# Asking for scratch stores through GpSimd's transfer queue instead of SyncE's

## The chip, the core and the metric

The kernel runs on one core of a Trainium2 chip. The core has a matrix engine (TensorE, in the profile PE, with its weight loads as PEld), a vector engine (VectorE, DVE), a scalar engine (ScalarE, ACT), GpSimd (POOL) and SyncE (SP). Each engine takes its own instructions strictly in order and waits on semaphores for the others. Transfers between the on-chip memory and the chip's main memory (HBM) are asked for by an instruction on one engine's queue, and are then carried by 16 DMA engines beside everything else. The metric is device time in microseconds of one execution.

## What is computed

One block of a streaming encoder on 1024 tokens of width 1024, all in float32, cut to what matters here:

```python
h = x + 0.5 * swiglu(rmsnorm(h, g1), W1)            # inner width 2816
u = rmsnorm(h, g2)
q, k, v, g_ret, p, gates = split(u @ w_in)          # 4 heads of 256
ret  = headnorm(retention(rotary(q), rotary(k), v)) * silu(g_ret)
pool = multiscale_pool(p, pool_w, pool_scale)       # trailing windows 2, 4, 8, 16
merged = sigmoid(gate0) * (ret @ w_ret_up) + sigmoid(gate1) * (pool @ w_pool_up)
h = h + merged @ w_out
h = h + 0.5 * swiglu(rmsnorm(h, g3), W2)
return rmsnorm(h, g_final)
```

## The kernel before

Activations lie on chip as tiles of 128 features by 1024 tokens. A float32 product is made of three matmuls: both operands are split into a high part, rounded to the matrix engine's format (ACT, line 161), and a low rest (DVE, line 162), and `mm3` (lines 181 to 183) multiplies high by high, high by low and low by high. Most matrix products are also cut by a Strassen scheme into seven block products instead of eight (`strassen`), and some into fewer still (`common`, lines 540 to 630). So DVE and ACT have much work beside PE: splits, sums and differences of blocks, and the evacuation of PE's result banks.

The stages run in this order: the first SwiGLU's inner products (`ffn_in`, tiles named `a...`), its outer product (`ffn_out`, `b...`), the projections (`values` with tiles `v...`, then `project` for q, k, g, p and the gates t), retention with the pooled branch's products as fillers (`retention`, `pool_up`), the merge (`two_groups`, `ru...`; `out_group`, `wo...`), the second SwiGLU (`c...`, `d...`), and the last norm.

Not everything fits on chip, so intermediate tiles go to scratch tensors in HBM and come back:

- `ffn_in` makes, for each of 11 pairs k of hidden tiles, four operands of the outer product and stores them: `B[k]` (`e["n"]`, line 797), `R[k]` and `T[k]` (`lo` and `hi`, after line 801), `T4[k]` (`e["m"]`, after line 806). `ffn_out` loads them: `p1` at first loads `R[k]` and then the weights `ra` (`bra`, `dra` in the trace); `p6` makes three sums of the weights on DVE (lines 906 to 908).
- `Next.quarter` keeps each new residual tile h (`h1` from `bacc`, `h2` from `wo`, line 311). The same tile is afterwards scaled in place by ACT (line 338, `r22`) and turned into operands.
- `project` stores q and k (`keep`), the swished g (`swish`), the two sigmoid gates (`gate`, line 1237, from small tiles `t0z` to `t7z`) and the pooled windows (`window`); `values` stores v, cut in rows of 1 KB (`store`).
- `pool_up` stores its gated product (`pm`), and the retention units their gated output (`ret`, line 1705).

Counted from the loops these are 88 stores in the two `ffn_in`, 32 of h, 16 of v, 16 of q and k, 8 of g, 32 of gates, 8 of pooled windows, 9 of `pm` and 8 of `ret`: 217, each of 256 or 512 KB.

All loads and all these stores go through one helper, `load` (line 140), which issues them on SP's queue. SP does nothing else. A store's tile lies in one of a few buffers that later tiles reuse, so whoever next writes the buffer waits until the store has landed.

What sets the order: the code states the work in a written order, in which `Flow` deals out side work between the matrix products. When the program is built, a planner places every instruction in its engine's queue by that order and by its own estimate of when the instruction can start; work under `soon()` goes first. On the chip each queue then runs in the order that was planned.

Of the kernel before, what the change touches and what calls it, by code (L numbers as in the profile page):

```python
# [90 lines left out]
def block_kernel(ctx: ExitStack, tc, x, x_tok, x_two, vecs, f1_in, f1_out, w_in, w_v, pool_w, w_ret, w_pool, w_o,  # L91
                 f2_in, f2_out, f2_far, g_row, rope, decay, consts, out, out_tok):
    nc = tc.nc
# [35 lines left out]
    def c2(name):  # L129
        return sb.tile([P, H], F32, tag="c2", bufs=N_C2, name=name)  # L130
# [7 lines left out]

    def load(dst, src):
        nc.sync.dma_start(dst, src)  # L140

    def eights(name):

        return sb.tile([P, 32], F32, tag="ss", bufs=2, name=name)[:, :8]
# [4 lines left out]
    def half(t, j):  # L149
        return t[:, j * H : (j + 1) * H]  # L150
# [146 lines left out]
    class Next(Norm):  # L297
# [9 lines left out]
        def quarter(self, mt, tokens, tile):  # L307
            src = tile[:, tokens]
            self.tiles[mt, tokens.start // H] = src
            if self.keep is not None:  # L310
                load(self.keep[mt][:, tokens], src)
            self.square(mt, tokens, src)

        def put(self, n, i, src, by=None):
# [426 lines left out]
    def ffn_in(nx, w, ops, name, start=None):  # L741

        R, T, B, T4 = ops
        hid = {}

        def group(g):
            gate_up = {}

            def dest(which):
                tile, j = which  # L750
                if tile not in gate_up:
                    gate_up[tile] = (tl if start and g == 0 else t4)(f"{name}{'gu'[tile]}{g}")
                return half(gate_up[tile], j)

            later = []

            def evac(which, in0, in1):
                tile, j = which
                dst, rms = dest(which), nx.rb
                if in1 is not None:  # L760
                    tt(dst, in0, in1, ADD)
                elif not tile and rms is not None:
                    tt(dst, in0, half(rms, j), MUL)
                    return
                else:
                    copy(dst, in0)
                if not tile:
                    later.append(j)

            def end():  # L770
                gate, up = gate_up[0], gate_up[1]

                def scale():
                    if len(later) == 2:
                        tt(gate, gate, nx.rms(), MUL)
                    else:
                        for j in later:
                            tt(half(gate, j), half(gate, j), half(nx.rms(), j), MUL)

                def times(j):  # L780
                    tt(half(up, j), half(gate, j), half(up, j), MUL)

                flow.add(scale, lambda: act(gate, gate, AF.Silu), lambda: times(0), lambda: times(1))
                hid[g] = up
                k = g % FH
                if g < FH:
                    return
                lo, hi, e = hid.pop(k), up, {}
                R11, R12, R21, R22 = half(lo, 0), half(lo, 1), half(hi, 0), half(hi, 1)

                def w1():

                    e["n"], e["m"] = gate, c2(f"{name}m{k}")
                    tt(half(e["n"], 0), R12, R11, SUB)

                def w1b():
                    tt(half(e["n"], 1), R22, R12, SUB)
                    load(B[k], e["n"])

                def w2():  # L800
                    tt(R12, R22, half(e["n"], 0), SUB)
                    load(R[k], lo)
                    load(T[k], hi)

                def w3():
                    tt(e["m"], R21, R12, SUB)
                    load(T4[k], e["m"])
                    done.add(k)

                flow.add(w1, w1b, w2, w3)  # L810

            if start and g == 0:
                return plain_group(nx, start, f"{name}{g}_", evac, end)
            return lambda shared: strassen(nx, w[g, 0], w[g, 1], f"{name}{g}_", evac, end, shared=shared, dest=dest)

        done = ops_done.setdefault(name, set())
        order = [g for k in range(FH) for g in (k, k + FH)]
        if start:

            return chain(group(0), pairs_of_both(nx, (group(g) for g in order[1:]), BY_OPERAND, 3))  # L820
        return pairs_of_both(nx, (group(g) for g in order), BY_OPERAND, 2)
# [320 lines left out]
    qs, ks, gs, pooled = (spill(n, KT) for n in ("q", "k", "g", "p"))  # L1142

    vs = spill("v", 4, 4 * H)
    gates = spill("gt", 2 * KT)
    pm, ret = spill("pm", KT), spill("ret", KT)
# [25 lines left out]
    def project(kind, n):  # L1172

        at = {"q": 0, "k": KT, "g": 3 * KT, "p": 4 * KT, "t": 5 * KT}[kind] + 2 * n
        name = f"{kind}{n}"
        pair = {}
# [44 lines left out]

        def keep(dst):
            for i in range(2):
                load(dst[2 * n + i], pair[i])
            stored.add(name)

        def swish(i):
            act(pair[i], pair[i], AF.Silu)
            load(gs[2 * n + i], pair[i])
            if i:  # L1230
                stored.add(name)

        def gate(i):
            mt = 2 * n + i
            for j in range(2):
                z = c2(f"{name}z{i}{j}")
                act(in_row(z), in_turns(half(pair[i], j)), AF.Sigmoid, bias=vec[:, V_B0 + mt : V_B0 + mt + 1])
                load(half(gates[mt], j), z)
            if i:
                stored.add(name)  # L1240

        def window(i):

            win = 2 << n
            t = {}

            def double(step):
                s = t.get("s", pair[i])
                o = t["s"] = t4(f"{name}s{i}_{step}")
                tt(o[:, step:], s[:, step:], s[:, : S - step], ADD)  # L1250
                copy(o[:, :step], s[:, :step])

            def mean():
                z, s = pair[i], t["s"]

                edge = sb.tile([P, 16], F32, tag="edge", bufs=2, name=f"{name}e{i}")
                tt(edge, s[:, :16], cst[:, C_CNT + 16 * n : C_CNT + 16 * n + 16], MUL)
                tt(edge, edge, z[:, :16], SUB)
                stt(s, s, 1.0 / win, z, MUL, SUB)
                copy(s[:, :16], edge)  # L1260
                load(pooled[2 * n + i], s)
                if i:
                    stored.add(name)

            return *(lambda b=b: double(1 << b) for b in range(n + 1)), mean
# [13 lines left out]
    def values():  # L1279
# [55 lines left out]

        def store(o, j, i, src):
            to = vs[2 * o + j].rearrange("p (h t c) -> p h t c", h=2, t=4)
            load(to[:, :, i], src.rearrange("p (h c) -> p h c", h=2))
            if i == 3:
                stored.update(f"v{h}{j}" for h in (2 * o, 2 * o + 1))  # L1340

# [101 lines left out]
    def pool_up():  # L1443
        gate, stores = {}, {}
        for mt in range(KT):

            def begin(mt=mt):
                await_stored(f"t{(KT + mt) // 2}")
                if mt < KT - 1:
                    r = raw(f"pg{mt}")  # L1450
                    load(r, gates[KT + mt])
                    gate[mt] = [half(r, j) for j in range(2)]
                    stores[mt] = [(pm[mt], r)]
                    return
                gate[mt] = [c2(f"pg{mt}{j}") for j in range(2)]
                for j, g in enumerate(gate[mt]):
                    load(g, half(gates[KT + mt], j))
                stores[mt] = [(half(pm[mt], j), g) for j, g in enumerate(gate[mt])]

            def evac(dst, mt=mt):  # L1460
                for j, g in enumerate(gate.pop(mt)):
                    tt(g, dst[j], g, MUL)
                for to, at in stores.pop(mt):
                    load(to, at)

            yield from plain(M.get, KT, w_pool[mt], f"pu{mt}", evac, begin,
                             (sum_bank, sum_bank if mt < 4 else bank))
# [41 lines left out]
    class Unit:  # L1509
# [185 lines left out]
        def finish(self):  # L1695
            for i in range(2):
                await_stored(f"g{self.h}")
                g = (t4 if self.h == 1 else tl)(f"rg{self.h}{i}")
                load(g, gs[2 * self.h + i])
                for nh in range(2):  # L1700
                    b = bank(f"ot{self.h}{nh}{i}")
                    for t in range(4):
                        o = t * HD + i * P
                        nc.tensor.transpose(b[:, t * P : (t + 1) * P], self.O[nh][:, o : o + P], ident)
                    tt(half(g, nh), b, half(g, nh), MUL)
                load(ret[2 * self.h + i], g)

    units = [Unit(h, nh) for h in range(NH) for nh in range(2)]
    up = Next("ru", None)
# [349 lines left out]
```

## Time and profile before

| | us |
|---|---|
| median of 3 runs | 2074.63 |
| lowest and highest of them | 2074.14, 2074.94 |
| the profiled execution, whole | 2073.32 |
| its span, first to last instruction | 2071.5 |
| outside the span | 1.8 |

| in the span | instructions on the engine | share of the span busy |
|---|---|---|
| PE matmuls | 10672 | 99% |
| PE weight loads | 10672 | 87% |
| DVE | 3262 | 89% |
| ACT | 2061 | 53% |
| transfers of SP's queue | 310.64 MB | 44.1% of the 16 DMA engines |

How to read the views: a row of the timeline gives start and duration in us, the engine, the line of the code, the operation, the tile that is written and those read, and in brackets how long the engine sat idle before it and what ended that. "SPq" is SP's queue; a row there is the issue of a transfer, not its movement. In the view of waits the three numbers are the total in us, how often, and the longest. Matmuls overlap, so a matmul's duration is longer than the step from one to the next.

### The profile page before, as it was taken

To read this page: it belongs to the slowest core of one execution; us is meant where nothing else is said; L and a number is where in the kernel's file an instruction comes from. 1 tells how busy PE (TensorE), PEld (TensorE's weight loads), DVE (VectorE), ACT (ScalarE), POOL (GpSimd) and SP (SyncE) were. 2 spreads that over 40 slices of the span, in tenths; PEclk is the share of its full clock that TensorE was granted. 3 is DMA by queue.
4 is the path that set the end of the run, shared out by engine and by line. 5 is a ranking of instruction groups with operands and counts; after the bars stand their busy time and mean duration, and the time that the engine had idled before them with its cause. 6 is when DMAs were issued, how large, how long until landed. Compare 5 with 4: busy or idle time off the path is not lost.

```text
span 2071.5 us, 29684 instructions
## 1 busy us (share of the span) xinstructions
PE 2046.9 (99%) x10672; PEld 1810.4 (87%) x10672; DVE 1835.4 (89%) x3262; ACT 1092.9 (53%) x2061; POOL 0.2 (0%) x4
## 2 busy tenths in 40 slices
PE   9999999999999999999999999999999999999998
PEld 7888999888888888888888999888789999988887
DVE  8799898997996799978878888999989989899897
ACT  8544454554653535444547763456645545455454
POOL 0000000000000000000000000000000000000000
PEclk9999999999999999999999999999999999999999
DMA  7232424585543333332436566724224232357642
GB/s 263 82 138 77 143 89 141 198 275 193 188 143 104 110 112 112 125 121 101 135 130 233 191 232 232 255 93 159 75 85 137 89 138 87 135 206 264 219 145 100
DMA packets 118819, 313.57 MB, mean 151 GB/s; under 512 B 13200, under 2 KB 17424, under 8 KB 118672
## 3 DMA queue, kind: packets, MB, share of 16 engines
q1 hardware_dynamic: 118096, 310.64, 44.1%
q8 instruction: 83, 1.36, 0.3%
q10 hardware_dynamic: 576, 1.05, 0.1%
q14 instruction: 64, 0.52, 0.1%
HBM read 220.93 MB, written 90.70 MB: 150 GB/s over the span
## 4 chain that ended last, share of the span: by engine, by line
PE 79%; DVE 15%; issue 2%; DMA 2%; ACT 1%; SPq 0%; ACTq 0%; DVEq 0%
PE c_b L181 2%; PE a_b L181 2%; PE c_b L182 2%; PE c_b L183 2%; PE a_b L182 2%; PE a_b L183 2%; PE c_e L183 2%; PE c_e L182 1%; PE c_e L181 1%; PE a_e L181 1%; PE a_e L183 1%; PE a_e L182 1%; PE c_a L183 1%; PE c_a L182 1%; PE c_a L181 1%
## 5 line engine op out<-in xcount | busy, mean ns | idle before, releaser
L182 PE MATMUL c_b<-n3T,c_wS 128*128 128x512 f32 x176 | 66.8, 380 | 0.0
L181 PE MATMUL c_b<-n3T,c_wS 128*128 128x512 f32 x176 | 66.5, 380 | 0.2 <-ACT n3T L161 0.2
L183 PE MATMUL c_b<-n3T,c_wS 128*128 128x512 f32 x176 | 66.7, 379 | 0.0
L181 PE MATMUL a_b<-n1T,a_wS 128*128 128x512 f32 x168 | 63.7, 379 | 0.0
L182 PE MATMUL a_b<-n1T,a_wS 128*128 128x512 f32 x168 | 63.7, 379 | 0.0
L183 PE MATMUL a_b<-n1T,a_wS 128*128 128x512 f32 x168 | 63.7, 379 | 0.0
L181 PE MATMUL a_a<-n1R,a_wL 128*128 128x512 f32 x120 | 45.5, 379 | 0.0
L183 PE MATMUL a_a<-n1R,a_wL 128*128 128x512 f32 x120 | 45.5, 379 | 0.0
L182 PE MATMUL a_a<-n1R,a_wL 128*128 128x512 f32 x120 | 45.5, 379 | 0.0
L182 PE MATMUL c_a<-n3R,c_wL 128*128 128x512 f32 x112 | 42.7, 381 | 1.1 <-DVE n3R L166 1.1
L181 PE MATMUL c_a<-n3R,c_wL 128*128 128x512 f32 x112 | 42.6, 380 | 0.7 <-ACT c_b L521 0.7
L183 PE MATMUL c_a<-n3R,c_wL 128*128 128x512 f32 x112 | 42.4, 379 | 0.0
L181 PEld LDWEIGHTS c_b<-n3T,c_wS 128*128 128x128 f32 x176 | 33.2, 189 | 5.1 <-ACT n3T L161 0.6
L182 PEld LDWEIGHTS c_b<-n3T,c_wS 128*128 128x128 f32 x176 | 33.3, 189 | 4.8 <-DVE n3T L162 0.3
L183 PEld LDWEIGHTS c_b<-n3T,c_wS 128*128 128x128 f32 x176 | 33.3, 189 | 4.6
L183 PEld LDWEIGHTS a_b<-n1T,a_wS 128*128 128x128 f32 x168 | 31.8, 189 | 4.5
L181 PEld LDWEIGHTS a_b<-n1T,a_wS 128*128 128x128 f32 x168 | 31.8, 189 | 4.4
L182 PEld LDWEIGHTS a_b<-n1T,a_wS 128*128 128x128 f32 x168 | 31.8, 189 | 4.4
L162 DVE TENSOR_TENSOR a_wS<-a_S,a_wS 128x512 fp32r<-128x512 f32 x45 | 30.6, 682 | 4.9 <-ACT a_wS L161 4.9
L161 ACT CAST c_wS<-c_S 128x512 fp32r<-128x512 f32 x46 | 27.8, 622 | 11.4 <-DVE c_S L484 7.0
L182 PE MATMUL c_e<-n3T,c_wL 128*128 128x512 f32 x88 | 33.5, 380 | 0.1
L181 PE MATMUL c_e<-n3T,c_wS 128*128 128x512 f32 x88 | 33.5, 380 | 0.0
(3159 smaller groups left out, 8002.1 us busy)
## 6 DMA issues: line engine op xcount, KB each, us to landing
c_ra<-in_f_in SPq DMA_DIRECT2D x22, 512.0 KB, 3.6
c_rb<-in_f_in SPq DMA_DIRECT2D x22, 512.0 KB, 3.8
a_ra<-in_f_in SPq DMA_DIRECT2D x21, 512.0 KB, 3.8
a_rb<-in_f_in SPq DMA_DIRECT2D x21, 512.0 KB, 3.8
t<-au SPq DMA_DIRECT2D x11, 512.0 KB, 2.8
b<-ag SPq DMA_DIRECT2D x11, 512.0 KB, 3.8
r<-au SPq DMA_DIRECT2D x11, 512.0 KB, 3.6
bra<-in_f_out SPq DMA_DIRECT2D x11, 512.0 KB, 5.4
```

What stands on the lines that cost most here:

```text
L161: copy(hi, src)
L162: tt(lo, src, hi.bitcast(F32), SUB)
L181: mm(dst, w[0], m[0], start=start, stop=False, skip_group_check=True)
L182: mm(dst, w[0], m[1], start=False, stop=False, skip_group_check=True)
L183: mm(dst, w[1], m[0], start=False, stop=stop, skip_group_check=True)
```

## The change

A second helper, `save`, issues a transfer on GpSimd's queue. The 217 stores into scratch memory call it instead of `load`. Loads stay on SP's queue, and so do the stores of the kernel's outputs (half of the token-major output stays on ACT's queue as before). No tile, buffer count, product or written order changes.

```diff
     def load(dst, src):
         nc.sync.dma_start(dst, src)
+
+    def save(dst, src):
+
+        nc.gpsimd.dma_start(dst, src)
...
             if self.keep is not None:
-                load(self.keep[mt][:, tokens], src)
+                save(self.keep[mt][:, tokens], src)
...
                     tt(half(e["n"], 1), R22, R12, SUB)
-                    load(B[k], e["n"])
+                    save(B[k], e["n"])
...
                     tt(R12, R22, half(e["n"], 0), SUB)
-                    load(R[k], lo)
-                    load(T[k], hi)
+                    save(R[k], lo)
+                    save(T[k], hi)
...
                     tt(e["m"], R21, R12, SUB)
-                    load(T4[k], e["m"])
+                    save(T4[k], e["m"])
...
-                load(dst[2 * n + i], pair[i])
+                save(dst[2 * n + i], pair[i])
...
-            load(gs[2 * n + i], pair[i])
+            save(gs[2 * n + i], pair[i])
...
-                load(half(gates[mt], j), z)
+                save(half(gates[mt], j), z)
...
-                load(pooled[2 * n + i], s)
+                save(pooled[2 * n + i], s)
...
-            load(to[:, :, i], src.rearrange("p (h c) -> p h c", h=2))
+            save(to[:, :, i], src.rearrange("p (h c) -> p h c", h=2))
...
                 for to, at in stores.pop(mt):
-                    load(to, at)
+                    save(to, at)
...
-                load(ret[2 * self.h + i], g)
+                save(ret[2 * self.h + i], g)
```

## The prediction

> **What bounds the kernel now.** First the page: its span, the busy shares and the chain of work that ended last.
>
> ```profile
> span 2071.5 us, 29684 instructions
> ...
> PE 2046.9 (99%) x10672; PEld 1810.4 (87%) x10672; DVE 1835.4 (89%) x3262; ACT 1092.9 (53%) x2061; POOL 0.2 (0%) x4
> ...
> PE 79%; DVE 15%; issue 2%; DMA 2%; ACT 1%; SPq 0%; ACTq 0%; DVEq 0%
> ```
>
> PE is busy for 2046.9 of 2071.5 us and carries 79% of the chain. DVE is next, and transfers are 2% of the chain. POOL does nothing. So an edit that removes no matmul can win at most the 24.6 us in which PE has none. The windows of 50 us tell where these lie.
>
> ```profile
> 0.00:50.00 50.00, 48.79 (x212) 39.62 (x213) 44.65 (x73) 43.55 (x78) 0.20 (x4) 1.00 0.75 262
> ...
> 400.00:450.00 50.00, 48.67 (x232) 42.63 (x231) 50.00 (x83) 25.67 (x44) 0.00 (x0) 1.00 0.79 268
> ...
> 1850.00:1900.00 50.00, 48.55 (x235) 42.61 (x235) 49.44 (x82) 25.36 (x44) 0.00 (x0) 1.00 0.77 269
> ...
> 2050.00:2071.50 21.50, 14.22 (x66) 11.83 (x64) 15.41 (x36) 7.91 (x19) 0.00 (x0) 0.94 0.51 195
> sum 2071.50, PE 2046.93 PEld 1810.45 DVE 1835.45 ACT 1092.90 POOL 0.20; mean PE 48.74 PEld 43.11 DVE 43.70 ACT 26.02 POOL 0.00
> ```
>
> The columns are length, then busy time and instructions of PE, PEld, DVE, ACT and POOL, then granted clock, share of the DMA engines and GB/s. PE lacks 1.2 us in the first row and 7.3 in the last, neither of which has a store into scratch near it. Some 16.1 us are left inside. The second and third row are the passage from `ffn_in` to `ffn_out` in the two SwiGLUs: 1.3 and 1.5 us missing there. In the view of PE's waits the largest, with what ended them, are:
>
> ```profile
> PE wo1b L181 <- ACT wo1wS L161: 1.7, 1, 1.7
> PE c_x L181 <- DVE cg L619: 1.5, 1, 1.5
> PE a_x L181 <- DVE ag L619: 1.3, 1, 1.3
> ...
> PE c_a L182 <- DVE n3R L166: 1.1, 2, 1.0
> ```
>
> PE waits for DVE or ACT, never for a transfer. A transfer counts only where DVE or ACT stood still for it just before.
>
> **Part 1: what stood behind a store.** The timeline of SP's queue at the two passages:
>
> ```profile
> 388.42 1.28 SPq L140 DMA_DIRECT2D bL22a<-in_f_out  x2
> 392.61 0.33 SPq L140 DMA_DIRECT2D m<-am  x1
> 392.99 0.93 SPq L140 DMA_DIRECT2D bra<-in_f_out  x2
> ...
> 1840.51 1.44 SPq L140 DMA_DIRECT2D dL22a<-in_f_out  x2
> 1844.71 0.33 SPq L140 DMA_DIRECT2D m<-cm  x1
> 1845.09 0.92 SPq L140 DMA_DIRECT2D dra<-in_f_out  x2
> ```
>
> And DVE's, around the first and at the second:
>
> ```profile
> 391.30 0.68 DVE L907 TENSOR_TENSOR bs<-bs,bra 128x512 f32<-128x512 f32 x1
> 391.91 0.68 DVE L806 TENSOR_TENSOR am<-au,au 128x512 f32<-128x512 f32 x1
> 392.51 0.68 DVE L908 TENSOR_TENSOR bs<-bra 128x512 f32<-128x512 f32 x1
> ...
> 398.22 0.69 DVE L906 TENSOR_TENSOR bs<-bra,bL22a 128x512 f32<-128x512 f32 x1 [1.42 <-DMA bra<-in_f_out]
> ...
> 1850.56 0.69 DVE L906 TENSOR_TENSOR ds<-dra,dL22a 128x512 f32<-128x512 f32 x1 [1.66 <-DMA dra<-in_f_out]
> ```
>
> SP had nothing to do from 389.70 (388.42 + 1.28). It stood at the store of `am` until DVE had made it (391.91 + 0.68 = 392.59). The weights `bra` behind it went out at 392.99, 0.05 us after the store's issue ended, so they waited for nothing of their own just then. DVE stood still 1.42 us for them, and PE missed 1.3 us soon after. The second passage is the same, with 1.66 and 1.5. With the store on POOL's queue SP goes straight on, and the weights can be asked for up to 3.3 us earlier (392.99 - 389.70), more than either idle time. What is late next is DVE itself, which is busy 50.00 of 50 us in that window. I take the whole of what PE missed, 1.3 + 1.5 = **2.8 us less**. The bounds are 0 (the buffer of `bra` free only just before) and 2.8.
>
> The other loads that stood behind stores had consumers that came later or that PE did not wait for, so I put nothing for them.
>
> **Part 2: the stores themselves.** They do not start earlier. The view of SP's own waits shows it standing at the stores:
>
> ```profile
> SPq L140 <- DVE am L806: 25.2, 11, 8.4
> SPq L140 <- DVE wo L1831: 23.9, 8, 8.5
> ...
> SPq L140 <- DVE wo L1833: 17.3, 8, 2.9
> ...
> SPq L140 <- DMA pm<-pg: 13.6, 6, 4.7
> ```
>
> For 11 of 11 stores of `am` and 16 of 16 of h from `wo` (two groups of eight), SP was there first and waited for the data. Such a store was issued 0.02 us after its data (392.59, 392.61) and gains nothing. What changes is how fast it lands from another queue. Rows of issues, the last number being the median from issue to landing:
>
> ```profile
> v<-vc SPq DMA_DIRECT2D x16, 256.0 KB, 3.4
> ...
> h<-wo SPq DMA_DIRECT2D x16, 256.0 KB, 2.0
> ...
> out<-n4o ACTq DMA_DIRECT2D x4, 256.0 KB, 2.6
> out<-n4o SPq DMA_DIRECT2D x4, 256.0 KB, 2.3
> ```
>
> No row has a store on POOL's queue. The nearest is the same output on ACT's and on SP's queue: 0.3 us later on the other one. The far end is what a store of the same size pays for a harder form, v against h: 1.4 us. That it lands sooner is bounded by the issue that SP's sequencer does, about 0.32 us:
>
> ```profile
> L140 SPq DMA_DIRECT2D h<-bacc x16: 319/323/327, 522.3 to 618.0; - x16
> ```
>
> So a store lands between 0.3 us sooner and 1.4 us later. I take the middle of the two late ends, 0.9 us, and keep both.
>
> A late landing costs only where someone waits for the tile. The gates are the clearest: one of those who waited for their stores, ACT's timeline, and PE's; below them ACT and DVE where they waited for h and v.
>
> ```profile
>   ACT g0p L543: 1.6, 1
> ...
> 778.55 1.57 ACT L1237 ACTIVATE t0z<-t0B,vec 128x512 f32<-128x512 f32 x2
> 780.02 0.57 ACT L526 COPY p3v<-p3b 128x512 f32<-128x512 f32 x1
> ...
> 780.64 0.48 PE L181 MATMUL p3b<-n2T,p3wS 128*128 128x512 f32 x1 [0.53 <-ACT p3v L526]
> ...
> 1415.97 0.72 ACT L338 ACTIVATE wo<-wo,vec 128x512 f32<-128x512 f32 x1 [0.27 <-DMA h<-wo]
> ...
> 660.03 1.39 DVE L1356 TENSOR_TENSOR vc<-vL,vf 128x512 f32<-128x512 f32 x2 [0.25 <-DMA v<-vc]
> ```
>
> Behind a sigmoid that waits for its small buffer stand, on ACT, the evacuations of PE's banks (lines 526, 543); PE missed 0.53 us for one. I find four such places: the gates that are made between the pooled groups (here, and once more in a later group), the scaling in place of h by ACT (line 338), which must wait for the store of the same tile, and v, where DVE waits for small tiles. At each, 0.9 us more meets some idle time of ACT or DVE; no row tells how much, so between all of it absorbed and none I charge PE one half: 4 x 0.9 / 2 = **1.8 us more**. Elsewhere PE has its distance: three matmuls on each of four tiles of a block product stand between a bank's last matmul and its next use.
>
> Stores that are read back (`pm` in the row above, `ret`) are late by the same 0.9 us, at 6 loads where SP waits for `pm`. DVE and ACT have their splits planned ahead of PE there, so I put nothing and leave it to the range.
>
> **Part 3: the queues.** SP is rid of 217 issues of about 0.32 us, some 70 us. Its share of the chain is 0%, so that is worth nothing by itself. POOL gets 217 issues and their waits, and has 2071 us for them; if it took the far end above, 1.4 us, for each, that is 304 us. Nothing else is queued there, so a store that waits for its data holds up only later stores, as it did on SP.
>
> **The sum.** 2073.32 - 2.8 + 1.8 = 2072.3 in terms of the profiled execution. That stood 1.3 below the median (2074.63), so **2073.6 us**. A measurement here can tell about 0.2%, 4.1 us, from no change.
>
> One thing the edit exposes is DVE's kind of work at the moment of an issue:
>
> ```profile
> L1693 DVE TENSOR_SCALAR o<-o,ir2r x8: 347/348/349, 1248.1 to 1249.9; 128x256 f32<-128x256 f32 x8
> ```
>
> Eight of these, a tensor with a scalar each, run in a row from 1248.1 to about 1250.2, 2.1 us, once per head and shortly before the stores of `ret`. If POOL could issue nothing meanwhile, four bursts would delay four groups of loads by 2.1 us each; with PE paying a quarter, that is 2.1 more. The Trainium skill, "SBUF — State Buffer", section "Who interferes with whom", speaks for that: the descriptors of a transfer on GpSimd's queue are written by GpSimd itself, which is locked out while DVE runs in a two-port mode, and tensor-with-scalar operations can enter one while a tensor with a tensor cannot. This trace has no transfer of POOL and cannot show it.
>
> **Rivals.**
>
> - *Replanned for the better.* L806 of one stage ran between L907 and L908, two lines that follow each other in the code: the queues are planned, and the plan changes when loads no longer stand behind stores. The 1.1 us of `n3R` and the 1.7 of `wo1` could go as well. For it: they are waits for the order on DVE and ACT. Against: DVE is nearly full in such stretches. Price: 2074.6 - 2.8 - 2.8 = 2069.0.
> - *Late landings win*, the slower side. Place: the gates and pooled windows of the four groups p, two halves each, where ACT's queue stands at a small buffer. Price: 8 x 1.4 = 11.2 with no idle time left to absorb it, so 2074.6 - 2.8 + 11.2 = 2083.0. It decides from the point where the added landing exceeds the idle time ahead of ACT's evacuation; at 780.64 there is none.
> - *Held issues*: POOL stands still during the bursts of L1693, for 2.1 us in all: 2073.6 + 2.1 = 2075.7.
> - *Nothing comes free.* The weights wait for their buffer after all, and the landings are absorbed: 2074.6.
>
> **How the numbers follow.** My forecast has 0.40, and its own range is 2070.5 to 2077.5. The better plan has 0.20, late landings 0.25, held issues 0.05 and nothing free 0.10. Faster by over 0.2% (below 2070.5) is the better plan: 0.20. Within 0.2%: 0.40 + 0.05 + 0.10 = 0.55. Slower: 0.25. The range reaches past the better plan and most of the way to the late landings: 2067.5 to 2082.0; about 0.05 lies below it and 0.15 above.
>
> **What would show it.** Part 1 is right if the timeline of SP has `bra` and `dra` issued with no store ahead, DVE's idle time of 1.42 and 1.66 is gone, and PE's waits for `a_x` and `c_x` with it. Part 2 is right if the issue rows of POOL show h landing in about 2.9 us instead of 2.0, and ACT's or DVE's waits for landings of `gt`, `h` and `v` grow; it is wrong if landings stay at 2.0, or go beyond 3.4. Part 3 is wrong if POOL is busy for more than a third of the span or stores start well after their data. The whole is wrong if PE's missing time grows at places where no store is near, which would be the plan, or if DVE's single operations get longer.

## The result and the profile after

| | before | after |
|---|---|---|
| median, us | 2075.08 (2074.14 to 2076.71, 6 runs) | 2090.78 (2086.12 to 2093.49, 6 runs) |
| profiled execution, whole | 2073.32 | 2091.86 |
| its span | 2071.5 | 2089.7 |

The changed kernel takes 1.0074 times as long, with a 95% interval of 1.0064 to 1.0084: 15.7 us slower by the medians, 18.2 by the spans of the profiled executions. The forecast was 2073.6 us, and the range ended at 2082.0.

The page of the changed kernel, its span, busy shares, the first two queues (packets, MB, share of the 16 DMA engines) and the chain:

```profile
span 2089.7 us, 29842 instructions
...
PE 2050.8 (98%) x10672; PEld 1813.0 (87%) x10672; DVE 1836.2 (88%) x3262; ACT 1092.3 (52%) x2061; POOL 119.4 (6%) x221
...
q1 hardware_dynamic: 84800, 224.11, 33.3%
q0 software_dynamic: 24592, 86.52, 10.5%
...
PE 63%; issue 22%; DVE 8%; DMA 4%; ACT 2%; POOL 1%; SPq 0%; POOLq 0%; ACTq 0%; DVEq 0%
```

The stores have moved: 86.52 MB on GpSimd's queue. DVE's busy time is the same within 1 us, and PE's has grown by 3.9. The chain's split changed much (issue 2% to 22%), but it says nothing of which wait is new; the view of PE's waits does:

```profile
PE g0b L185 <- ACT g0v L530: 2.6, 1, 2.6
PE wo2a L185 <- ACT wo2b L525: 2.3, 1, 2.3
PE ru1a L185 <- ACT ru1b L525: 2.1, 1, 2.1
PE t5b L185 <- ACT t5v L530: 1.7, 1, 1.7
PE t6b L185 <- ACT t6v L530: 1.7, 1, 1.7
PE wo1b L185 <- ACT wo1wS L165: 1.7, 1, 1.7
PE ru0a L185 <- ACT ru0b L525: 1.6, 1, 1.6
PE t7b L185 <- ACT t7v L530: 1.6, 1, 1.6
```

In the changed file every line behind the new helper is 4 higher: 530 and 525 are the evacuations 526 and 521 of before. Of these eight only `wo1b` was there before. The gates' four (t5b, t6b, t7b, g0b) make 7.6 us, `ru` 3.7, `wo2a` 2.3, and two further down at `ob` 2.1 (1.4 and 0.7): together 15.7. The waits of 1.5 and 1.3 for `c_x` and `a_x` are gone. A part of the rest is in the granted clock, the last number but two of each row of the windows (after the name of the stretch: length, then busy time and instructions of PE, PEld, DVE, ACT, POOL, then clock, share of the DMA engines, GB/s):

```profile
1046.00:1050.00 4.00, 3.77 (x10) 3.02 (x11) 3.54 (x6) 1.21 (x3) 0.00 (x0) 0.57 0.00 0
...
1415.50:1418.40 2.90, 2.83 (x7) 2.30 (x8) 2.90 (x6) 2.12 (x4) 0.00 (x0) 0.50 0.00 0
```

Behind the wait for g0b, and behind that at `wo1b`, PE ran at about half its clock: 4.00 x 0.43 + 2.90 x 0.50 = 3.2 us lost. (Before, the same wait at `wo1b` was followed by a clock of 1.00.) So 15.7 + 3.2 - 2.8 = 16.1 of the 18.2 us have a place; the rest is in small growths, such as 0.5 to 1.0 us at `p3b`. Not all of it is a store that holds a buffer: just before the wait at `ob` near 1208 us, ACT stood still 2.92, 1.18 and 2.08 us for loads of q and k (0.85 and 0.17 at that place before).

One of the four gate stalls shows the whole chain. The timeline of the changed kernel, with SP's and POOL's queues, ACT and PE:

```profile
922.48 0.33 SPq L140 DMA_DIRECT2D q2ra<-in_w_in  x1
...
924.51 0.33 SPq L140 DMA_DIRECT2D q2rb<-in_w_in  x1
...
925.92 0.54 POOL L144 DMA_DIRECT2D gt<-t4z  x1 [1.19 <-ACT t4z L1241]
926.99 0.84 ACT L1241 ACTIVATE t4z<-t4B,vec 128x512 f32<-128x512 f32 x1 [1.47 <-DMA gt<-t4z]
...
930.30 0.58 ACT L547 COPY t5p<-t5e 128x512 f32<-128x512 f32 x1 [1.44 <-DMA gt<-t4z]
931.58 0.58 ACT L530 COPY t5v<-t5b 128x512 f32<-128x512 f32 x1 [0.69 <-DMA gt<-t4z]
...
932.22 0.48 PE L185 MATMUL t5b<-n2T,t5wS 128*128 128x512 f32 x1 [1.73 <-ACT t5v L530]
```

The same place before:

```profile
921.47 0.36 SPq L140 DMA_DIRECT2D q2ra<-in_w_in  x1
...
922.83 2.79 SPq L140 DMA_DIRECT2D gt<-t4z  x3
...
925.71 0.40 SPq L140 DMA_DIRECT2D q2rb<-in_w_in  x1
...
927.12 0.59 ACT L526 COPY t5v<-t5b 128x512 f32<-128x512 f32 x1 [0.20 <-DMA gt<-t4z]
```

The evacuations `t5p` and `t5v` write into small tiles of the same eight buffers that the gates' tiles `t4z` lie in, so they wait until a gate has landed. Before, the second half of the next weights (`q2rb`) stood behind the last store of the four and went out at 925.71. After, it is asked for at 924.51, ahead of two of the four stores. The store issued at 925.92 took 5.6 us to land; its counterpart before took 2.5. ACT stands, then PE. Before, ACT had already waited 0.20 us here: there was no room left.

### The profile page after: what moved, and what is told of

Same layout as the page of the kernel before. It is cut to its first block, busy times and chain, and to the rows that moved or that the text cites. A ratio compares the mean times of both kernels' runs of the same rounds, so it can differ in the third digit from the quotient of the medians.

```text
span 2089.7 us, 29842 instructions
## 1 busy us (share of the span) xinstructions
PE 2050.8 (98%) x10672; PEld 1813.0 (87%) x10672; DVE 1836.2 (88%) x3262; ACT 1092.3 (52%) x2061; POOL 119.4 (6%) x221
## 3 DMA queue, kind: packets, MB, share of 16 engines
q0 software_dynamic: 24592, 86.52, 10.5%
## 4 chain that ended last, share of the span: by engine, by line
PE 63%; issue 22%; DVE 8%; DMA 4%; ACT 2%; POOL 1%; SPq 0%; POOLq 0%; ACTq 0%; DVEq 0%
PE c_b L185 2%; PE c_b L186 2%; PE a_b L185 2%; PE c_b L187 2%; PE a_b L186 2%; PE a_b L187 2%; PE c_e L187 2%; PE c_e L186 2%; PE c_e L185 2%; PE a_e L185 2%; PE a_e L186 2%; PE a_e L187 2%; PE a_a L186 1%; PE a_a L187 1%; PE a_a L185 1%
## 5 line engine op out<-in xcount | busy, mean ns | idle before, releaser
L166 DVE TENSOR_TENSOR c_wS<-c_S,c_wS 128x512 fp32r<-128x512 f32 x46 | 31.9, 696 | 2.4 <-ACT c_wS L165 2.3
```

What stands on the lines that cost most here:

```text
L166: tt(lo, src, hi.bitcast(F32), SUB)
```

## Experiments

Each kernel ran beside runs of before on the same chip; the ratio is to those, and their medians were 2073.2, 2074.0 and 2074.4 us in the three sessions. Lines are those of the changed file.

**Two halves of the change.** First only the 88 stores of the two `ffn_in`:

```diff
-                    load(B[k], e["n"])
+                    save(B[k], e["n"])
...
-                    load(R[k], lo)
-                    load(T[k], hi)
+                    save(R[k], lo)
+                    save(T[k], hi)
...
-                    load(T4[k], e["m"])
+                    save(T4[k], e["m"])
```

> Only the 88 stores of the two inner SwiGLU products (B, R, T, T4) go to GpSimd's queue; the other 129 stay on SyncE's. Theory (the gain is the weights that no longer stand behind the last of these stores, and the loss is later landings of the stores that someone waits for, which these are not): the two PE waits at the passages go (1.5 + 1.6 us) and nothing comes, so about 2072, 3 us less than before. Rival (GpSimd's queue harms every store, or the new plan of the queues does it): these are 40% of the stores and half of the bytes, so some 6 to 8 us slower than before, about 2082.

Measured: 2071.63 us, ratio 0.9991 (0.9982 to 0.9999), span 2069.7. The waits for `a_x` and `c_x` are gone, and of the eight waits shown above only `wo1b` is there. Part 1 of the prediction stands, though the gain is about 1.6 us by the medians and 1.8 by the spans instead of 2.8: two waits that before does not have, 0.6 at `bp5a` and 0.7 at `s`, take some of it back. Where these come from was not traced.

Then only the other 129:

> The complement: only the 129 stores outside the two inner SwiGLU products go to GpSimd's queue. Theory (late landings of these): all of the loss and none of the gain, 18.2 + 3.1 = about 21 us slower than before, 2096 and slower than the full change. Rival (every store harms alike): about 60% of the full change's 16 us, 2085.

Measured: 2091.26 us, ratio 1.0087 (1.0074 to 1.0101), some 5 us less than the 2096 expected; the interval overlaps that of the full change, so that it is slower than that is not shown. It has most of the stalls of the changed kernel (t5b 1.9, t6b 1.6, t7b 1.4, g0b 1.7, wo2a 2.2 in the view of waits, but 1.1 for `ru` instead of 3.7), and `a_x` and `c_x` again with 1.9 and 1.5. The loss lies in these 129 stores.

**The gates alone**, 32 stores, one line:

```diff
-                load(half(gates[mt], j), z)
+                save(half(gates[mt], j), z)
```

> Only the 32 gate stores go to GpSimd's queue. Theory (a gate's store that lands late keeps ACT's small buffers and so the evacuation of PE's bank): the four PE waits behind ACT's line 530 near 930, 968, 1005 and 1043 us return with 1.8 to 2.7 us each, and about 1 us more in the groups before them, in all 8 to 9.5 us slower, 2084. Rival (the waits come from other stores or loads that were moved): 0 to 2 us, 2075 to 2077.

Measured: 2082.68 us, ratio 1.0044 (1.0031 to 1.0058). The gates t4z to t7z land in 4.3 to 5.0 us (median of each group of four), before in 2.9 to 4.2. So 32 stores bring more than half as much as the whole change, but not all at the places expected. The four waits are there with 1.2, 1.1, 0.8 and 0.8 us, not 1.8 to 2.7 each, and the largest new one lies at a pooled group: PE stood 2.5 us at `p0y`, after ACT had stood 3.94 us for the landing of a `t2z`. The changed kernel has 0.2 at `p0y`; how the loss spreads over the places depends on what else moves.

**The gates on ACT's queue** instead, which is a queue of the same kind as SP's (hardware_dynamic in the page of the profile, where GpSimd's is software_dynamic):

```diff
-                load(half(gates[mt], j), z)
+                nc.scalar.dma_start(half(gates[mt], j), z)
```

> The same 32 gate stores on ScalarE's own queue instead, the rest on SyncE's as before. Theory A (a second queue has to share the 16 DMA engines with the loads of SyncE's queue, whichever engine asks): the gates land in 4.5 to 6 us in the groups t4 to t7 as they do from GpSimd, and the time is 5 to 9 us above before, 2080 to 2084. Theory B (the cost is GpSimd's own way of asking, about 0.65 us per store and more when several are in flight): they land in 2.5 to 4 us as from SyncE and the time is within 1.5 us of before, about 2075.5.

Measured: 2080.65 us, ratio 1.0032 (1.0019 to 1.0045). Nearly as slow, so it isn't GpSimd's way alone. But the two theories each got half: the time is that of A, and the landings are those of B, with medians of 2.7, 3.7, 2.7 and 2.6 us for t4z to t7z. PE's waits are 2.5 us at `t3b`, 1.9 at `t6b` and 1.0 at `g0b`. And the run tells less than it was meant to: an issue on ACT's queue waits in ACT's own order, behind instructions that themselves wait for a landing. Of t5z, the two stores that lay beside the loads of `k2ra` and `k2rb` took 5.1 and 5.7 us, the two after them 2.0 and 2.3. That put the loads under suspicion.

**Loads and stores in one queue again, GpSimd's.** First for every block product of `strassen`:

```diff
-            load(ra, wa)
-            load(rb, wb)
+            save(ra, wa)
+            save(rb, wb)
```

together with the stores of q, k, g, p, v and the gates, and the weights of v.

> The stores of q, k, g, p, v and the gates, and the weight loads of the same block products, go together through GpSimd's queue; everything else is as before. So the stores have GpSimd's slower way, but their weight loads stand in the same queue again instead of running beside them. Theory 'shared engines' (a store lands late because loads on another queue run at the same time): the gates t4z to t7z land in about 3.2 to 4.7 us (2.9 to 4.2 of before, plus 0.3), less than the 4.3 to 5.0 of the gates alone on GpSimd, the four stalls at t5b, t6b, t7b and g0b are each under 0.7 us, and the time is 2073 to 2077 us. Theory 'GpSimd's own way': they land in 4.3 us or more all the same, the four stalls stay at 1.0 us or more each, and the time is 2081 us or more.

Measured: 2092.88 us, ratio 1.0092 (1.0078 to 1.0105). The landings and the four stalls came out as "shared engines" said (3.2 to 3.7 us, and no wait left at t5b, t6b, t7b and g0b), and the time did not: the edit reaches more than the stage. The same function loads the weights of both SwiGLUs, of `ru` and of `wo`, whose neighbours stayed on SP's queue. PE waits 3.1 us at `ru0a`, 2.6 at `wo2a` and 1.6 at the start of the first SwiGLU, each followed by a granted clock of about half. At `wo` this made, unasked, the reverse case: the stores of h on SP's queue as before, the loads beside them on GpSimd's. The row of the transfers there and ACT's timeline:

```profile
wo3rb<-in_w_o POOLq DMA_DIRECT2D x1, 512.0 KB, 7.0
h<-wo SPq DMA_DIRECT2D x1, 256.0 KB, 7.0
```

```profile
1434.23 0.72 ACT L342 ACTIVATE wo<-wo,vec 128x512 f32<-128x512 f32 x1 [3.89 <-DMA h<-wo]
```

A store that SP issued took 7.0 us, and its counterpart before, in one queue with these loads, 3.3. PE's wait at `wo2a` came with it (2.6 us), with no store of h on GpSimd's queue. Two runs then made the pair cleanly, for the weights of p, t, q, k and g alone:

```diff
-            load(ra, wa)
-            load(rb, wb)
+            (save if name[0] in "pqkgt" and name[1:].isdigit() else load)(ra, wa)
+            (save if name[0] in "pqkgt" and name[1:].isdigit() else load)(rb, wb)
```

With the stores of q, k, g, the gates and the pooled windows beside them on GpSimd's queue:

> The run with one queue moved also the weight loads of a, ru and wo, whose stores stayed on the sync engine's queue. Here only those of p, t, q, k and g move, with the stores of the same groups (q, k, g, the gates, the pooled windows) beside them in GpSimd's queue; all else is as before. Theory 'shared engines': no load runs on another queue beside these stores, so the gates t4z to t7z land in 3.2 to 3.8 us, the stalls at t5b, t6b, t7b, g0b, ru0a and wo2a are all absent, and the time is 2073 to 2077 us. Theory 'GpSimd's own way is the price': 2081 us or more.

Measured: 2076.73 us, ratio 1.0012 (1.0003 to 1.0022). The gates' transfers between 915 and 1050 us (count, KB, median us to landing):

```profile
gt<-t4z POOLq DMA_DIRECT2D x4, 256.0 KB, 3.2
gt<-t5z POOLq DMA_DIRECT2D x4, 256.0 KB, 4.0
gt<-t6z POOLq DMA_DIRECT2D x4, 256.0 KB, 3.2
gt<-t7z POOLq DMA_DIRECT2D x4, 256.0 KB, 4.5
```

Two groups went above the 3.8 expected, and PE waited 0.3 us at t6b and less at the other three. The 2.3 us by which this run still lies above before are not shown to be the price of GpSimd's own way: PE's waits at `a_x` and `vL`, outside the transfers that moved, are 0.8 and 0.9 us longer than in the profile of before, and half a clock behind `wo1b` took some 1.7. And the reverse, every store on SP's queue, only these loads on GpSimd's:

> The reverse: every store stays on the sync engine's queue, as before; only the weight loads of p, t, q, k and g go through GpSimd's queue. No store has GpSimd's way. Theory 'shared engines': the gates land in 4 to 6 us though the sync engine issues them, the stalls at t5b, t6b, t7b and g0b appear with about 1 us each or more, and the time is 2079 to 2084 us. Theory 'GpSimd's own way is the price': the gates land in 2.9 to 4.2 us as before, those four stalls are absent, and the time is 2073 to 2076 us.

Measured: 2087.96 us, ratio 1.0064 (1.0050 to 1.0078); slower than expected, with stalls at t1b and p0y (1.3 and 1.6 us) besides. The same view, and PE's waits:

```profile
gt<-t4z SPq DMA_DIRECT2D x4, 256.0 KB, 5.3
gt<-t5z SPq DMA_DIRECT2D x4, 256.0 KB, 5.3
gt<-t6z SPq DMA_DIRECT2D x4, 256.0 KB, 5.2
gt<-t7z SPq DMA_DIRECT2D x4, 256.0 KB, 5.7
```

```profile
PE t5b L185 <- ACT t5v L530: 2.0, 1, 2.0
PE t7b L185 <- ACT t7v L530: 1.9, 1, 1.9
PE t6b L185 <- ACT t6v L530: 1.9, 1, 1.9
PE g0b L185 <- ACT g0v L530: 1.8, 1, 1.8
```

No store touches GpSimd here, and the four stalls are there, 7.6 us as in the changed kernel. At these gates this settles it: a store lands late because the loads no longer stand in its queue, whichever of the two has moved.

**Taking the wait away.** The gates on GpSimd's queue, their small tiles in four large buffers that nothing else uses in that stage:

```diff
-                z = c2(f"{name}z{i}{j}")
+                z = half(tl(f"{name}z{i}{j}"), 0)
```

> The 32 gates alone go through GpSimd's queue, and their small tiles lie in four large buffers that nothing else uses in that stage, so that a tile is free again one group later whatever its store does. Theory 'the wait for the buffer is the price': the gates still land in 4 to 5 us, no bank is evacuated late for them, the stalls at t5b, t6b, t7b and g0b are gone, and the time is that of before or up to 2 us less, 2071 to 2074 us, instead of 2082.7. Rival 'transfers of two queues slow the loads or the engines themselves': half of the loss or more stays, 2078 us or more.

Measured: 2071.86 us, ratio 0.9989 (0.9980 to 0.9998). The time is as expected and the four stalls are gone, but one part missed: the gates did not go on landing late.

```profile
gt<-t4z POOLq DMA_DIRECT2D x4, 256.0 KB, 2.3
gt<-t5z POOLq DMA_DIRECT2D x4, 256.0 KB, 2.3
```

With a place of their own the sigmoids no longer wait for an earlier gate, so they ran 17 to 41 us earlier than with the gates alone on that queue (the four of t4z went out from 882.88 to 912.67 us instead of 923.94 to 929.67, and the loads `q2ra` and `q2rb` only at 918.86 and 920.84) and met no load. So the run shows that the shared buffer is needed for the loss, and can't show late landings that cost nothing.

The same line in the changed kernel:

> The changed kernel with one line different: the gates' small tiles lie in the four large buffers. Theory 'the wait for the buffer is the price': the four stalls at t5b, t6b, t7b and g0b go (8.3 us), and with the long one the half-speed matmuls behind it (1.7 us), so 2079 to 2083 us; the stalls at ru0a, ru1a and wo2a stay. Rival: the late stores find another waiter in that stage, 2087 us or more.

Measured: 2075.30 us, ratio 1.0007 (0.9998 to 1.0016): no difference from before that can be told. By the two ratios that is some 14 us less than the changed kernel, more than the 8 to 12 that were expected. PE's largest waits in it:

```profile
PE wo2a L185 <- ACT wo2b L525: 2.5, 1, 2.5
PE ru1a L185 <- ACT ru1b L525: 1.8, 1, 1.8
PE wo1b L185 <- ACT wo1wS L165: 1.7, 1, 1.7
```

Of the three that the line does not touch, `ru1a` and `wo2a` stayed, as the theory says, and are paid for in part by the waits for `a_x` and `c_x` that went. The third, 1.6 us at `ru0a`, went though it was expected to stay, and the waits at `ob` fell from 2.1 to 0.4 us; why was not traced.

**The other two places by themselves.** The stores of `pm` and `ret` alone (lines 1468 and 1710), then those of h alone (line 315):

> Only the stores of pm and ret (32 and 8) go through GpSimd's queue. Theory: the two stalls of PE at ru0a and ru1a, 4.0 us in the changed kernel, are theirs, since the pairs of ret are stored last and read back first; so 2077 us, with ret landing in 5 us or more. Rival: those stalls came from what the rest of the change moved ahead of them; then 2073 to 2074 us.

Measured: 2078.00 us, ratio 1.0020 (1.0010 to 1.0029). PE waits 1.9 and 1.8 us at `ru0a` and `ru1a`. The large `pm` stores land in 5.8 us and `ret` in 5.6, against 2.9 and 4.5 before. (The expectation miscounts: `pm` has 9 stores, not 32.) The stalls are theirs; that they come through the read-back of `ret` is argued, and no view here follows it.

> Only the stores of h, the kept residual stream, go through GpSimd's queue (16 of one stage and 16 of another). Theory: the stall of 2.5 us at wo2a comes from them, through the scaling in place that waits for the store of the same tile; so 2075.5 us. They run beside few loads, so they land in 2.3 to 2.6 us instead of 2.0. Rival: 0.3 us later is absorbed and the stall belongs to the rest of the change: 2073 us.

Measured: 2078.84 us, ratio 1.0022 (1.0012 to 1.0031), more than expected; the wait at `wo2a` is 2.8 us, and some 1.7 us went with half a clock behind the wait at `wo1b`, a wait that before has too, in its profile without the half clock (see the end). The landing was expected to grow by 0.3 us, and that holds for the median of the 16. It does not hold for the one that matters. SP's and POOL's queues:

```profile
1411.93 0.33 SPq L140 DMA_DIRECT2D wo2ra<-in_w_o  x1
1412.54 0.33 SPq L140 DMA_DIRECT2D wo2rb<-in_w_o  x1
1413.14 0.33 SPq L140 DMA_DIRECT2D wo3ra<-in_w_o  x1
1414.34 0.33 SPq L140 DMA_DIRECT2D wo3rb<-in_w_o  x1
1415.32 0.54 POOL L144 DMA_DIRECT2D h<-wo  x1 [16.79 <-DVE wo L1837]
```

Before, SP's queue ran:

```profile
1412.54 0.33 SPq L140 DMA_DIRECT2D h<-wo  x1
1412.92 0.42 SPq L140 DMA_DIRECT2D wo3ra<-in_w_o  x1
```

Before, each of the two loads of `wo3` stood behind a store of h. Now all four loads, 2 MB, are asked for ahead of the store, and it lands after 6.3 us instead of 3.3. This is the plainest view of what the edit does.

**The best of it.** The 88 stores of `ffn_in` and the gates through GpSimd's queue, the gates in their own buffers:

> The two edits that each came out 0.1% below before, together: the 88 stores that had held up the weights go through GpSimd's queue, and so do the gates, whose small tiles lie in four large buffers of their own. Theory: the gains add, since they lie in different stages (1.5 to 2 us at each, 401 and 1854 us, for the stores; 1 to 2 us between 750 and 1050 us for the gates): 2068.5 to 2070.5 us. Rival: a gate wait had hidden something else, so only one of them shows: 2071.5 to 2072.

Measured: 2069.11 us, ratio 0.9974 (0.9964 to 0.9984): faster than both kernels. The two gains add at least: 5.3 us (by the interval 3.3 to 7.5), where the edits alone gave 1.6 and 2.1. No run has the gates in their own buffers with their stores on SP's queue, so whether GpSimd's queue has a part in the second gain, or the buffers alone make it, stays open.

## Why the prediction was wrong

**What bounds the kernel** held: PE, and a transfer counts only through DVE or ACT. PE's lost time grew at places where a store is near.

**Part 1** held in mechanism. `bra` now goes out right behind `bL22a`:

```profile
386.50 1.02 SPq L140 DMA_DIRECT2D bL22a<-in_f_out  x2
387.58 1.25 SPq L140 DMA_DIRECT2D bra<-in_f_out  x2
```

DVE no longer waits for it or for `dra`, and PE's waits at `a_x` and `c_x` are gone. By the run with these stores alone it is worth some 1.6 to 1.8 us, where 2.8 stood in the sum: the whole of what PE missed was taken, and new waits of 0.6 and 0.7 us elsewhere were not reckoned with. What it left out is the other side of the same coin: loads that no longer stand behind stores now go ahead of them or run beside them, everywhere else too.

**Part 2 is the step that failed**, in its bounds first. "A store lands between 0.3 us sooner and 1.4 us later" came from rows in which the stores had SP's queue to themselves or shared it with the loads. A store that meets no load does land 0.3 us later from its issue (2.3 against 2.0, in the run with h alone), and goes out about 0.4 us after its data instead of 0.03; that small step was well sized. The other bound failed too: the stores of v landed in 2.8 us from GpSimd's queue against 3.4 from SP's, 0.6 us sooner. Where loads run on the other queue it is 3 us and more: 5.6 against 2.5 for a gate, 5.9 to 6.3 against 3.3 for h. The row that would have told so was in the trace: behind the store of h at 1412.54 stood a load at 1412.92, and at the gates the load of 925.71. The part asked who waits behind a store on SP, found two passages where that hurts, and did not ask of the others what the waiting had protected.

Its places failed second. "I find four such places", "gates that are made between the pooled groups", with half charged at each: the loss sat at the gates after the pooled groups, t4z to t7z, where ACT had 0.20 us of waiting for `gt` before, so no slack at all. (The pooled groups were no empty guess: with the gates alone moved, `p0y` took 2.5 us.) "Elsewhere PE has its distance" failed at the same four. Scaling in place (line 338) was named rightly and cost 2.3 us instead of 0.45. "I put nothing and leave it to the range" for `pm` and `ret` cost 3.7 us.

**Part 3** held: POOL was busy 6% of the span, and stores went out 0.40 us after their data in the middle, at most 0.72 but for five of v (up to 2.2). The chain gives POOL 1%.

**The rivals.** Late landings was the right case, priced at 8 x 1.4 = 11.2 us and placed at the pooled groups; it was 15.7 us of waits at nine other places, and where the runs separate the two, at the gates, its size came from loads, not from GpSimd. The better plan did not come: the order on PE is nearly that of before, and where the four gate stalls lie it is the same. Held issues were not put to the test: in the changed kernel no issue on POOL lies within 1.5 us of the bursts of that line (now 1697; they would have delayed stores, not loads, since no load is on POOL's queue). An issue on POOL takes 0.53 to 0.55 us in nearly every group, 0.68 for v with its short rows.

The Trainium skill, "DMA: Bandwidth & Descriptors", section "Issuing engines are not separate DMA queues", says that transfers started by different engines run on the same 16 DMA engines and interleave, and that several issuers save only the time of issuing. The trace agrees with the first half: in the run with one queue, `wo3rb` asked for at 1426.95 and the store of h asked for at 1427.18 both took 7.0 us. Of the second half the runs show that it leaves something out: a second issuer can cost, since it undoes an order on which buffers were relying. Whether a late store is slow because it shares the engines with the other queue's loads, or because these were asked for before it, these runs do not separate in full. One row of the changed kernel speaks against the second alone: the store of `t4z` issued at 922.21 was asked for 0.27 us ahead of `q2ra`, with no issue on SP's queue since 905 us, and still took 4.8 us; before, the first store of `t4z` with `q2ra` 0.79 us behind it took 3.3.

## What to carry to other kernels

A queue in which loads stand behind stores is also a priority: it holds back loads that nobody needs yet, and the store lands sooner while someone waits for its buffer. Before splitting it, look at each store for the load that was behind it and for the slack of whoever reuses the buffer; move only stores that hold up a load that is late, or give the tile a buffer that nobody waits for. Price a landing by rows with loads under way, not by the median of quiet ones.

## What the hardware showed unexpectedly

PE's granted clock fell to about half for some 3.4 us after some of the waits, so that a wait cost up to 1.7 us more than its length; in the run with one queue it was twice that behind 3.1 us at `ru0a` (granted clock 0.93 from 1322 to 1327 us and 0.57 from 1327 to 1334). Its length doesn't decide: in the changed kernel it fell behind 2.6 us at g0b and not behind 2.3 at `wo2a`; in the run with the loads apart behind 2.0 at t5b and 1.9 at t7b, and not behind 1.9 at t6b and 1.8 at g0b; with h alone not behind 2.8 at `wo2a`; with the gates alone not behind 2.5 at `p0y`. The wait of 1.7 us at `wo1b`, which all kernels have, was followed by it in the profiles of five of them and not in that of before. So a single profile may hold 1.7 us that another of the same kernel lacks (inferred, since each kernel has one profile here), and a stall can be worth more than the view of waits says. The Trainium skill, "TensorE: Matmul & The Clock Gate", section "Part 1: The HAM clock gate (the "warmup" mystery)", tells of a free-running window of 3.4 us, and of half a clock after at least one idle window of about that length. The time spent at half speed and the absence of a fixed threshold agree; but here waits of 1.7 to 2.6 us were enough.
